# GpSimd takes over the softmax scalings and the recurrence tree's products in a hybrid decoder block

## The chip, the cores and the metric

The kernel runs on one core of one Trainium2 chip. Its time is device microseconds of one execution. A core has five engines with queues of their own, each worked off in order: TensorE (PE; its weight loads are shown as PEld), VectorE (DVE), ScalarE (ACT), GpSimd (POOL) and SyncE (SP), which only starts transfers here.

## What is computed

Two layers of a hybrid decoder over 256 tokens of width 1024, in float32. Each layer projects the normalized input, runs three groups of heads side by side, projects their outputs back and adds a squared-ReLU feed-forward. Cut to what matters here:

```python
for layer in range(DEPTH):
    h = _rmsnorm(x, norm1_g[layer])
    proj = h @ w_in[layer]
    o_a = _hgrn2(aq, af, ai, ag, ...)          # gated linear recurrence, 4 heads, 64x64 state
    o_b = _nsa(bq, bkc, bvc, ...)              # compressed + selected + window attention, 8 heads
    o_c = _fox(cq, ck, cv, cf, ...)            # forgetting attention, 4 heads
    x = x + concatenate([o_a, o_b, o_c]) @ w_o[layer]
    h2 = _rmsnorm(x, norm2_g[layer])
    x = x + square(relu(h2 @ w_up[layer])) @ w_down[layer]
...
# the recurrence: scores decayed by the product of the forget gates between s and t
decay = exp(where(causal, G[t] - G[s], NEG_BIG))         # G = cumsum(log f)
scores = einsum('bhtk,bhsk,bhtsk->bhts', q, k, decay)
...
# every softmax of the attention groups
p = where(mask, exp(logits - m), 0.0)
return p / maximum(sum(p), TINY)
```

## The kernel before

Tokens lie in two tiles of 128 partitions. Every large matmul is done as three passes over a high and a low part (`mm3`, lines 229 to 231), so each weight tile of 128x1024 is loaded (`raw`), copied to `whi` by ScalarE (line 223) and has its low part `wlo` subtracted by VectorE (line 224). A projection matmul below is one of these passes over 256 columns; a weight tile of the projections feeds 24 of them.

The recurrence is computed as a tree of seven levels, `a_level(0)` to `a_level(6)` (t0 to t6 below). Level `lv` multiplies queries and keys of neighbouring blocks of 2^lv tokens on TensorE into the one bank `pa` (line 470), which is emptied into `AT` by VectorE (line 479, under a mask) or, from level 5 on, by ScalarE (line 477). Then the queries `Qbd` are multiplied by the decays `Th` in two halves (line 485), the keys `Kc` once (line 487; `Kc` and the forget gates lie in buffers tagged `m2`, so the rows show `m`), and the decays themselves are paired for the next level (line 490). The next level's matmuls read the new `Qbd` and `Kc`. `a_out` ends the tree (lines 495 to 513).

The sparse attention group has heads b0 to b7, the forgetting group c0 to c3. A head's scores (lines 821 and 822, or 874 to 876) go through a masked maximum on VectorE (line 751) and an exponential with a running sum on ScalarE (line 161). The reciprocal sums, times the gates, are `rr`. `scale` then multiplies the probabilities `pt_` (buffers tagged `big0`, `big` in the rows) in place, in four pieces for a b head (two of 128 and two of 256 columns) and two for a c head (128 and 256). `SCALE_ACT` lists which pieces ScalarE scales (four of the six kinds), VectorE does the others. The scaled probabilities are transposed on TensorE (lines 836, 841, 884) into one of two banks `tr`, copied out and multiplied with the values (lines 858, 895). The compressed branch goes from `Z` and `w1` (line 613) over `hidT` (line 640) and `KC` (lines 652 to 659) to its scores (line 772).

The order of the steps in the program is the table `ORDER`, in which the tree's levels, the heads and the projections (`+ai`, `+q1`, ...) are mixed. What finally stands in each engine's queue is decided by the framework's list scheduler when the program is built: it follows that order as a priority and lets a later step go first where it reckons an earlier one is not ready. Where an operation sits on another engine, the scheduler reckons with another duration, and so the queues of all engines may come out in another order.

Of the kernel before, what the change touches and what calls it, by code (L numbers as in the profile page):

```python
# [13 lines left out]
AF = mybir.ActivationFunctionType  # L14
ALU = mybir.AluOpType
# [3 lines left out]
P = 128  # L19
# [38 lines left out]
WO_LAST = (0, 1, 2, 3)  # L58


WBUFS = (4, 6, 5)
SCALE_ACT = (1, 3, 4, 5)
CHUNK_N = {n: sum(b - a for a, b in c) for n, c in CHUNKS}
CHUNK_OFF = {}
_o = 0
# [70 lines left out]
def tile_block(ctx: ExitStack, tc: tile.TileContext, x_in, win, wo, wup, wdn, w1, vec, cst, out, dbg=None):  # L136
    nc = tc.nc
    V, A, G, PE = nc.vector, nc.scalar, nc.gpsimd, nc.tensor
# [31 lines left out]
    def T(shape, dt=F32, tag=None, bufs=1, pool=None):  # L170
        cnt[0] += 1
        return (pool or apool).tile(shape, dt, name=f"{tag}_{cnt[0]}", tag=tag, bufs=bufs)
# [3 lines left out]
    def bank(tag):  # L176
        return T([P, 512], F32, tag, BANKS[tag], pp)
# [163 lines left out]
    for L in range(DEPTH):  # L341
# [115 lines left out]
        th = [fT]  # L457

        def a_level(lv):


            Th = th[0]
            h = 1 << lv
            nb = S // (2 * h)
            ps = bank("pa")
            for t in range(2):
                for p in range(2):
                    o = (t * 2 + p) * P
                    mv = Qbd[:, p, :, t * P:(t + 1) * P].rearrange("p a (b two h) -> p a b two h", two=2, h=h)[:, :, :, 1, :]
                    PE.matmul(ps[:, o:o + P].rearrange("p (a b h) -> p a b h", a=2, h=h),  # L470
                              Kc[:, p, t * P:(t + 1) * P], mv, start=True, stop=True)
            atv = AT.rearrange("p a (b two h) -> p a b two h", two=2, h=h)[:, :, :, 1, :]
            psv = ps.rearrange("p (a b h) -> p a b h", a=8, h=h)
            if h >= 32:
                for b in range(64 // h):
                    r = slice(2 * h * b, 2 * h * b + h)
                    A.activation(atv[r, :, b, :], psv[r, :, b, :], AF.Copy)
            else:
                V.copy_predicated(
                    atv, hm[:, lv, :].rearrange("p (b h) -> p b h", h=h)[:, None, :, :].to_broadcast([P, 8, 64 // h, h]), psv)  # L480
            tv = Th.rearrange("p a (b two) -> p a b two", two=2)
            for a in range(2):
                r = slice(64 * a, 64 * a + 64)
                qv = Qbd[r, :, a, :].rearrange("p a (b two h) -> p a b two h", two=2, h=h)[:, :, :, 1, :]
                V.tensor_mul(qv, qv, tv[r, :, :, 0][:, :, :, None].to_broadcast([64, 2, nb, h]))
            kv = Kc.rearrange("p a (b two h) -> p a b two h", two=2, h=h)[:, :, :, 0, :]
            V.tensor_mul(kv, kv, tv[:, :, :, 1][:, :, :, None].to_broadcast([P, 2, nb, h]))
            if lv < 6:
                th[0] = T([P, 2, P], tag="Th", bufs=2)[:, :, :nb]
                V.tensor_mul(th[0], tv[:, :, :, 0], tv[:, :, :, 1])  # L490

        def a_out():
            ps = bank("pa")
# [254 lines left out]
        def softmax_part(ps, mask, n, ptile, o, nmx, sm):  # L748

            dst = ptile[:, o:o + n]  # L750
            V.tensor_tensor_reduce(out=dst, in0=ps, in1=mask, scale=-1.0, scalar=3.0e38,  # L751
                                   op0=ALU.add, op1=ALU.min, accum_out=nmx)
            act_exp(dst, dst, AF.Exp, bias=nmx, scale=-1.0, accum_out=sm)

        def scale(p, r, on_act):
            if on_act:
                A.activation(p, p, AF.Copy, scale=r)
            else:
                V.tensor_scalar(p, p, r, None, ALU.mult)

        PCT = [None, None]

# [49 lines left out]
        def head_b(g, j):  # L812
            hd = g * 4 + j
            pair, par = hd // 2, hd % 2
            pt_ = T([P, 768], tag="big0", bufs=4)
            nmx = T([P, 4], tag="nmx", bufs=4)
            sm = T([P, 4], tag="sm", bufs=4)
            for t, c0, n in ((0, P, 256), (1, 0, 512)):
                ps = bank("sc")
                sl = slice(t * P, (t + 1) * P)  # L820
                PE.matmul(ps[:, :n], qS[par][:, pair, sl], KS[:, g, c0:c0 + n], start=True, stop=False)
                PE.matmul(ps[:, :n], qS[par][:, pair, sl], KLB[:, g, c0:c0 + n], start=False, stop=True)
                w = n // 2
                for b, m in enumerate((tri, tri) if t == 0 else (m_tz, m_zt)):
                    i = 2 * t + b
                    softmax_part(ps[:, b * w:b * w + w], m, w, pt_, 256 * t + b * w, nmx[:, i:i + 1], sm[:, i:i + 1])
            r = T([P, 4], tag="rr", bufs=4)
            V.reciprocal(r, sm)
            rv = r.rearrange("p (t b) -> p t b", t=2)
            V.tensor_mul(rv, rv, gv[:, :, 1:3, g, j])  # L830
            for i, (o, n) in enumerate(((0, P), (P, P), (256, 256), (512, 256))):
                scale(pt_[:, o:o + n], r[:, i:i + 1], i in SCALE_ACT)

            ps0 = bank("tr")
            for i, o in enumerate((0, 384, P, 512)):
                PE.transpose(ps0[:, i * P:(i + 1) * P], pt_[:, o:o + P], ident)
            p0 = T([P, 2, S], tag="P0", bufs=3)
            A.activation(p0.rearrange("p b t -> p (b t)"), ps0, AF.Copy)
            ps1 = bank("tr")
            for i, o in enumerate((256, 640)):  # L840
                PE.transpose(ps1[:, i * P:(i + 1) * P], pt_[:, o:o + P], ident)
            p1 = T([P, 2, P], tag="P1", bufs=3)
            A.activation(p1.rearrange("p b t -> p (b t)"), ps1[:, 0:S], AF.Copy)
            PT[hd] = (p0, p1)
# [20 lines left out]
        def head_c(hd):  # L865
            u_, e_ = hd // 2, hd % 2
            pt_ = T([P, 768], tag="big0", bufs=4)
            nmx = T([P, 4], tag="nmx", bufs=4)
            sm = T([P, 4], tag="sm", bufs=4)
            for t in range(2):  # L870
                n = P * (t + 1)
                sl = slice(t * P, (t + 1) * P)
                ps = bank("sc")
                PE.matmul(ps[:, :n], cqS[e_][:, u_, sl], CK[:, hd, 0:n], start=True, stop=False)
                PE.matmul(ps[:, :n], cqS[e_][:, u_, sl], KLC[:, hd, 0:n], start=False, stop=False)
                PE.matmul(ps[:, :n], sel_r[:, hd:hd + 1].to_broadcast([P, P]), CC[:, 0:n], start=False, stop=True)  # L876
                softmax_part(ps[:, :n], tri if t == 0 else m_zt, n, pt_, t * P, nmx[:, t:t + 1], sm[:, t:t + 1])
            r = T([P, 4], tag="rr", bufs=4)
            V.reciprocal(r[:, 0:2], sm[:, 0:2])
            for t, (o, n) in enumerate(((0, P), (P, 256))):  # L880
                scale(pt_[:, o:o + n], r[:, t:t + 1], t + 4 in SCALE_ACT)
            ps0 = bank("tr")
            for i in range(3):
                PE.transpose(ps0[:, i * P:(i + 1) * P], pt_[:, i * P:(i + 1) * P], ident)
            p0 = T([P, 2, S], tag="P0", bufs=3)
            p0f = p0.rearrange("p b t -> p (b t)")
            A.activation(p0f[:, 0:384], ps0[:, 0:384], AF.Copy)
            PTC[hd] = p0f
# [55 lines left out]
        def wo_step(i):  # L944
# [12 lines left out]
        }  # L957
        step = {
            "t": a_level, "w": b_compress, "kc": b_compressed, "a_out": a_out,
            "cb": b_cmp_branch, "b": lambda i: head_b(i // 4, i % 4), "pb": lambda i: pv_b(i // 2, i % 2),  # L960
            "c": head_c, "pc": pv_c, "forget": c_forget, "wo": wo_step,
        }
        for name in ORDER:
# [163 lines left out]
```

## Time and profile before

| what | us |
|---|---|
| runs, median of 3 (lowest to highest) | 698.83 (697.93 to 699.84) |
| the profiled execution | 699.06 |
| its span, first to last instruction | 697.3 |
| mean granted TensorE clock | 0.993 of full |

The profile is of one execution. Its span begins with the first instruction of the program and ends with the last; the execution's own time is 1.8 us longer. In the rows, times are microseconds from the span's start. A mean granted clock below 1.00 in a stretch says that TensorE ran part of it at the lower of its two levels, 1.2 instead of 2.4 GHz. In rows of a timeline the first number is the start, the second the time taken, and brackets tell how long the engine stood idle before it and which work ended that.

### The profile page before, as it was taken

To read this page: it belongs to the slowest core of one execution; us is meant where nothing else is said; L and a number is where in the kernel's file an instruction comes from. 1 tells how busy PE (TensorE), PEld (TensorE's weight loads), DVE (VectorE), ACT (ScalarE), POOL (GpSimd) and SP (SyncE) were. 2 spreads that over 40 slices of the span, in tenths; PEclk is the share of its full clock that TensorE was granted. 3 is DMA by queue.
4 is the path that set the end of the run, shared out by engine and by line. 5 is a ranking of instruction groups with operands and counts; after the bars stand their busy time and mean duration, and the time that the engine had idled before them with its cause. 6 is when DMAs were issued, how large, how long until landed. Compare 5 with 4: busy or idle time off the path is not lost.

```text
span 697.3 us, 11902 instructions
## 1 busy us (share of the span) xinstructions
PE 675.9 (97%) x4578; PEld 602.4 (86%) x4578; DVE 451.6 (65%) x987; ACT 398.0 (57%) x761; POOL 10.9 (2%) x28
## 2 busy tenths in 40 slices
PE   6999989999999999999999999899999999999997
PEld 5998979768988998899799988786799988998896
DVE  5878788838655545654587897786567456545552
ACT  7654675887444434554457556688865445444440
POOL 3100000000100000000000000000000000000000
PEclk9999998999999999999999999999999999999999
DMA  8852561206566666666546418421266666666631
GB/s 289 265 153 73 174 189 49 73 1 211 168 203 181 181 185 183 192 182 194 153 128 213 150 31 260 133 62 31 86 190 180 184 191 196 180 185 181 185 118 61
DMA packets 31017, 108.88 MB, mean 156 GB/s; under 512 B 3568, under 2 KB 4080, under 8 KB 30960
## 3 DMA queue, kind: packets, MB, share of 16 engines
q1 hardware_dynamic: 30960, 108.11, 51.5%
q8 instruction: 36, 0.59, 0.3%
q14 instruction: 21, 0.17, 0.1%
HBM read 107.05 MB, written 1.05 MB: 155 GB/s over the span
## 4 chain that ended last, share of the span: by engine, by line
PE 82%; DVE 8%; ACT 5%; DMA 3%; issue 1%; SPq 0%; ACTq 0%
PE sc L229 9%; PE sc L230 9%; PE sc L231 9%; PE acc L229 9%; PE acc L231 8%; PE acc L230 8%; PE pv L230 3%; PE pv L231 3%; PE pv L229 3%; DMA raw<-in_win_dram 3%; PE pa L231 3%; PE pa L230 3%; PE pa L229 3%; DVE wlo L224 2%; PE pv L858 2%; PE sc L613 1%
## 5 line engine op out<-in xcount | busy, mean ns | idle before, releaser
L224 DVE TENSOR_TENSOR wlo<-raw,whi 128x1024 fp32r<-128x1024 f32 (+2 forms) x197 | 235.2, 1197 | 139.1 <-PE sc L231 67.2
L223 ACT ACTIVATE whi<-raw 128x1024 fp32r<-128x1024 f32 (+2 forms) x197 | 204.3, 1041 | 195.1 <-PE sc L230 73.3
L229 PE MATMUL sc<-kt,whi 128*128 128x256 f32 x512 | 145.1, 283 | 0.0
L231 PE MATMUL sc<-kt,wlo 128*128 128x256 f32 x512 | 144.9, 283 | 0.0
L230 PE MATMUL sc<-kt,whi 128*128 128x256 f32 x512 | 144.8, 283 | 0.0
L229 PEld LDWEIGHTS sc<-kt,whi 128*128 128x128 f32 x512 | 98.0, 191 | 1.0 <-ACT s L1015 0.3
L230 PEld LDWEIGHTS sc<-kt,whi 128*128 128x128 f32 x512 | 98.1, 192 | 0.6
L231 PEld LDWEIGHTS sc<-kt,wlo 128*128 128x128 f32 x512 | 98.1, 192 | 0.0
L229 PE MATMUL acc<-whi,kt 128*128 128x256 f32 (+2 forms) x288 | 88.9, 309 | 2.7 <-ACT whi L223 2.7
L231 PE MATMUL acc<-whi,kt 128*128 128x256 f32 (+2 forms) x288 | 88.4, 309 | 0.2
L230 PE MATMUL acc<-wlo,kt 128*128 128x256 f32 (+2 forms) x288 | 87.4, 305 | 0.0
L229 PEld LDWEIGHTS acc<-whi,kt 128*128 128x128 f32 x288 | 56.8, 197 | 5.3 <-ACT whi L223 3.3
L231 PEld LDWEIGHTS acc<-whi,kt 128*128 128x128 f32 x288 | 56.3, 196 | 3.3 <-DVE kt L239 1.1
L230 PEld LDWEIGHTS acc<-wlo,kt 128*128 128x128 f32 x288 | 56.3, 196 | 1.5 <-DVE wlo L224 0.4
L229 PE MATMUL acc<-whi,big 128*128 128x512 f32 x128 | 50.7, 396 | 0.0
L230 PE MATMUL acc<-wlo,big 128*128 128x512 f32 x128 | 50.6, 395 | 0.0
L231 PE MATMUL acc<-whi,big 128*128 128x512 f32 x128 | 50.5, 394 | 0.0
L161 ACT ACTIVATE big<-big,nmx 128x128 f32<-128x128 f32 (+1 forms) x80 | 35.6, 447 | 16.4 <-DVE nmx L751 16.3
L1016 DVE TENSOR_TENSOR s<-s 128x512 f32<-128x512 f32 x32 | 22.0, 688 | 24.1 <-ACT s L1015 24.1
L751 DVE CUSTOM_DVE_ANT_0 big<-sc,cst 128x128 f32<-128x128 f32 (+1 forms) x80 | 26.5, 349 | 8.0 <-PE sc L876 4.2
L1015 ACT ACTIVATE s<-sc 128x512 f32<-128x512 f32 x32 | 18.8, 588 | 18.7 <-PE sc L231 18.7
L231 PEld LDWEIGHTS acc<-whi,big 128*128 128x128 f32 x128 | 24.1, 188 | 5.8
(299 smaller groups left out, 1183.3 us busy)
## 6 DMA issues: line engine op xcount, KB each, us to landing
raw<-in_wup_dram SPq DMA_DIRECT2D x64, 512.0 KB, 3.6
raw<-in_wdn_dram SPq DMA_DIRECT2D x64, 512.0 KB, 3.6
raw<-in_win_dram SPq DMA_DIRECT2D x44, 512.0 KB, 4.5
raw<-in_wo_dram SPq DMA_DIRECT2D x16, 512.0 KB, 3.9
raw<-in_w_dram SPq DMA_DIRECT2D x8, 512.0 KB, 3.6
raw<-in_win_dram SPq DMA_DIRECT2D x4, 426.0 KB, 3.7
out_dram<-x SPq DMA_DIRECT2D x4, 256.0 KB, 2.0
raw<-in_win_dram SPq DMA_DIRECT2D x2, 284.0 KB, 2.7
```

What stands on the lines that cost most here:

```text
L161: r = A.activation(*a, **k)
L223: A.activation(hi[:, c0], raw[:, c0], AF.Copy)
L224: V.tensor_sub(lo[:, c0], raw[:, c0], hi[:, c0].bitcast(F32))
L229: PE.matmul(ps, ah, wh, start=start, stop=False)
L230: PE.matmul(ps, ah, wl, start=False, stop=False)
L231: PE.matmul(ps, al, wh, start=False, stop=stop)
L613: PE.matmul(pre_[0][64 * w:64 * w + 35, 0:P], Z[:, w].rearrange("p g m -> p (g m)")[:, j:j + 273:8], raw1[w][:, c0:c0 + P], start=(j == 0) ...
L751: V.tensor_tensor_reduce(out=dst, in0=ps, in1=mask, scale=-1.0, scalar=3.0e38, op0=ALU.add, op1=ALU.min, accum_out=nmx)
L858: PE.matmul(po[64 * e_:64 * e_ + 64, t * P:S], VS[:, t, bi * 2 + g, :], PT[g * 4 + jj * 2 + e_][t][:, bi, :], start=False, stop=False)
L1015: A.activation(rl, pu[i], AF.Relu)
L1016: V.tensor_mul(rl, rl, rl)
```

## The change

`scale` always uses GpSimd, for all 24 heads of both layers; the list `SCALE_ACT` goes. In `a_level` the two products on `Qbd`, the one on `Kc` and the one that pairs the decays go from VectorE to GpSimd. Nothing else of the source changes.

```diff
 WBUFS = (4, 6, 5)
-SCALE_ACT = (1, 3, 4, 5)
...
-                V.tensor_mul(qv, qv, tv[r, :, :, 0][:, :, :, None].to_broadcast([64, 2, nb, h]))
+                G.tensor_mul(qv, qv, tv[r, :, :, 0][:, :, :, None].to_broadcast([64, 2, nb, h]))
...
-            V.tensor_mul(kv, kv, tv[:, :, :, 1][:, :, :, None].to_broadcast([P, 2, nb, h]))
+            G.tensor_mul(kv, kv, tv[:, :, :, 1][:, :, :, None].to_broadcast([P, 2, nb, h]))
             if lv < 6:
                 th[0] = T([P, 2, P], tag="Th", bufs=2)[:, :, :nb]
-                V.tensor_mul(th[0], tv[:, :, :, 0], tv[:, :, :, 1])
+                G.tensor_mul(th[0], tv[:, :, :, 0], tv[:, :, :, 1])
...
-        def scale(p, r, on_act):
-            if on_act:
-                A.activation(p, p, AF.Copy, scale=r)
-            else:
-                V.tensor_scalar(p, p, r, None, ALU.mult)
+        def scale(p, r):
+            G.tensor_scalar(p, p, r, None, ALU.mult)
...
-                scale(pt_[:, o:o + n], r[:, i:i + 1], i in SCALE_ACT)
+                scale(pt_[:, o:o + n], r[:, i:i + 1])
...
-                scale(pt_[:, o:o + n], r[:, t:t + 1], t + 4 in SCALE_ACT)
+                scale(pt_[:, o:o + n], r[:, t:t + 1])
```

Since the list scheduler orders all queues anew, instructions move on TensorE, VectorE and ScalarE too; SyncE's queue stays as it was. In the changed kernel a line's number is lower by two up to `scale` and by five behind it (the tree's matmuls are L468 there, the scores L816 and L817, the heads' transposes L831 and L836, the `w1` matmuls L611). Three places in layer 0 are shown; layer 1 has the same order.

TensorE from t2 (bank pa_848) to t3 (pa_859), before; 22 projection matmuls and the four score matmuls of head b2 stand between t1 and t2, and all the rows left out are projection matmuls:

```order
L470 MATMUL pa_848<-Qbd_74,m_41_175 128x128 x4
L821 MATMUL sc_917<-KS_77,qS_179 128x256
L822 MATMUL sc_917<-KLB_78,qS_179 128x256
L230 MATMUL acc_984<-wlo_988,kt_16_100 128x256
L231 MATMUL acc_984<-whi_987,kt_17_101 128x256
...
L821 MATMUL sc_924<-KS_77,qS_179 128x512
L822 MATMUL sc_924<-KLB_78,qS_179 128x512
...
L470 MATMUL pa_859<-Qbd_74,m_41_175 128x128 x4
L836 MATMUL tr_902<-cst_70,big_156_878 128x128
```

The same place in the changed kernel; before the first row stand 8 projection matmuls and the four score matmuls of head b2 since t1:

```order
L468 MATMUL pa_848<-Qbd_74,m_41_175 128x128 x4
L229 MATMUL acc_984<-whi_987,kt_17_101 128x256
L227 MATMUL acc_984<-whi_987,kt_16_100 128x256
L228 MATMUL acc_984<-wlo_988,kt_16_100 128x256
L816 MATMUL sc_917<-KS_77,qS_179 128x256
L817 MATMUL sc_917<-KLB_78,qS_179 128x256
...
L468 MATMUL pa_859<-Qbd_74,m_41_175 128x128 x4
L816 MATMUL sc_924<-KS_77,qS_179 128x512
L817 MATMUL sc_924<-KLB_78,qS_179 128x512
L611 MATMUL sc_950<-raw_951,Z_177 35x128
```

Fourteen projection matmuls went from before t2 to behind the tree, and t3 moved up: between t2 and t3 six projection matmuls and one pair of scores are left, between t3 and t4 one pair of scores and eight of line 613.

TensorE around t4 (pa_963) before; between the rows left out stand only matmuls of line 613, and the transposes of the next head, b1 (tr_938), come only after t4, behind eight projection matmuls:

```order
L836 MATMUL tr_902<-cst_70,big_156_878 128x128
L613 MATMUL sc_950<-raw_951,Z_177 35x128
L836 MATMUL tr_902<-cst_70,big_156_878 128x128 x3
L841 MATMUL tr_909<-cst_70,big_156_878 128x128 x2
...
L470 MATMUL pa_963<-Qbd_74,m_41_175 128x128 x4
```

The same place in the changed kernel:

```order
L468 MATMUL pa_963<-Qbd_74,m_41_175 128x128 x2
L831 MATMUL tr_902<-cst_70,big_156_878 128x128
L468 MATMUL pa_963<-Qbd_74,m_41_175 128x128
L831 MATMUL tr_902<-cst_70,big_156_878 128x128 x3
L836 MATMUL tr_909<-cst_70,big_156_878 128x128 x2
L468 MATMUL pa_963<-Qbd_74,m_41_175 128x128
L611 MATMUL sc_950<-raw_951,Z_177 35x128
L831 MATMUL tr_938<-cst_70,big_166_914 128x128
...
L831 MATMUL tr_938<-cst_70,big_166_914 128x128 x3
L836 MATMUL tr_945<-cst_70,big_166_914 128x128 x2
```

The transposes of both heads now stand inside and right behind t4, with three matmuls of line 613 between them; 34 projection matmuls follow five more of line 613.

GpSimd from the products of t3 to those of t4 in the changed kernel (before, its queue holds nothing between the tables of rotations of layer 0, `tabc`, and those of layer 1):

```order
L483 TENSOR_TENSOR Qbd_74<-Qbd_74,Th_857 64x2x16x8 x2
L485 TENSOR_TENSOR m_41_175<-m_41_175,Th_857 128x32x8
L488 TENSOR_TENSOR Th_972<-Th_868 128x2x8
L754 TENSOR_SCALAR big_156_878<-big_156_878,rr_895 128x128 x2
L754 TENSOR_SCALAR big_156_878<-big_156_878,rr_895 128x256 x2
L754 TENSOR_SCALAR big_166_914<-big_166_914,rr_931 128x128 x2
L754 TENSOR_SCALAR big_166_914<-big_166_914,rr_931 128x256 x2
L483 TENSOR_TENSOR Qbd_74<-Qbd_74,Th_868 64x2x8x16 x2
```

The eight scalings of heads b2 and b1 stand between t3's products and t4's; they came here from VectorE's and ScalarE's queues, the products from VectorE's.

## Rows read from the trace of the kernel before

**Rows 1.** The page's busy times: us (share of the span) xinstructions of each engine.

```profile
PE 675.9 (97%) x4578; PEld 602.4 (86%) x4578; DVE 451.6 (65%) x987; ACT 398.0 (57%) x761; POOL 10.9 (2%) x28
```

**Rows 2.** TensorE's waits over the whole span: us in total, times, longest.

```profile
PE sc L640 <- DVE hidT L638: 2.7, 2, 1.5
...
PE sc L772 <- DVE KC L659: 2.3, 2, 1.1
PE pa L470 <- DVE m L487: 1.9, 3, 0.7
PE tr L841 <- ACT P L838: 1.4, 2, 0.7
PE tr L652 <- DVE s L552: 0.8, 2, 0.4
```

**Rows 3.** Stretches: length, busy time of each engine, granted clock, DMA share, GB/s.

```profile
105.00:125.00 20.00, 19.69 (x128) 17.21 (x128) 16.96 (x69) 12.44 (x33) 0.00 (x0) 0.83 0.26 81
125.00:140.00 15.00, 14.95 (x86) 11.32 (x86) 11.91 (x54) 13.65 (x44) 0.00 (x0) 1.00 0.12 35
...
440.00:460.00 20.00, 17.78 (x130) 16.50 (x128) 16.99 (x68) 12.31 (x33) 0.00 (x0) 0.91 0.26 79
```

**Rows 4.** Timeline of TensorE, layer 0, from t1 to the compressed branch's scores.

```profile
61.83 1.14 PE L470 MATMUL pa<-Qbd,m 128*128 128x128 f32 x8 [0.67 <-DVE m L487]
62.72 0.37 PE L229 MATMUL acc<-whi,kt 128*128 128x256 f32 x1
62.93 0.28 PE L230 MATMUL acc<-wlo,kt 128*128 128x256 f32 x1
63.05 0.28 PE L231 MATMUL acc<-whi,kt 128*128 128x256 f32 x1
...
66.82 1.13 PE L470 MATMUL pa<-Qbd,m 128*128 128x128 f32 x8 [0.53 <-DVE m L487]
...
73.73 1.16 PE L470 MATMUL pa<-Qbd,m 128*128 128x128 f32 x8
...
77.81 1.98 PE L613 MATMUL sc<-raw,Z 128*35 128x128 f32 x32
79.72 1.16 PE L470 MATMUL pa<-Qbd,m 128*128 128x128 f32 x8
...
92.04 1.03 PE L495 MATMUL pa<-Qbd,m 128*128 128x256 f32 x4
...
104.98 1.89 PE L772 MATMUL sc<-KC,qS 128*128 128x32 f32 x8 [1.13 <-DVE KC L659]
```

**Rows 5.** Timeline of VectorE, layer 0: t1's last product, and t4's bank.

```profile
66.25 0.42 DVE L487 TENSOR_TENSOR m<-m,Th 128x256 f32<-128x256 f32 x1
...
74.93 0.72 DVE L479 COPY_PREDICATED AT<-hm,pa 128x512 f32<-128x512 uint8 x1 [0.38 <-PE pa L470]
```

**Rows 6.** ScalarE's scalings, line 757: durations (ns min/median/max), and who waited (us, times).

```profile
L757 ACT ACTIVATE big<-big,rr x48: 385/448/511, 70.6 to 496.3; 128x128 f32<-128x128 f32 x24, 128x256 f32<-128x256 f32 x24
...
  PEld tr L836: 3.0, 8
  PEld tr L884: 0.8, 2
```

**Rows 7.** Timeline of GpSimd over the whole span.

```profile
2.52 0.31 POOL L207 MEMSET LF<- 128x256 f32 x1
2.77 0.21 POOL L207 MEMSET hidT<- 128x128 f32 x1
...
17.48 1.38 POOL L935 TENSOR_TENSOR tabk<-cst,vec 128x64 f32<-128x64 f32 x1
...
177.73 0.32 POOL L935 TENSOR_TENSOR tabk<-cst,vec 128x64 f32<-128x64 f32 x1
178.01 0.25 POOL L939 TENSOR_TENSOR tabc<-cst,vec 64x32 f32<-64x32 f32 x1
```

**Rows 8.** Timeline of VectorE from 15.5 us: weight subtractions beside GpSimd's product.

```profile
17.47 2.48 DVE L224 TENSOR_TENSOR wlo<-raw,whi 128x1024 fp32r<-128x1024 f32 x2
```

## Prediction

> **What bounds the kernel now.** I read the page's busy times first. TensorE is busy 675.9 of 697.3 us, VectorE 451.6, ScalarE 398.0, GpSimd 10.9 [rows 1]. So the span is TensorE's work plus what it waits, and no edit off TensorE can win more than TensorE's idle time and what a low clock costs it. Where that lies is read from stretches, not from the mean. The edits touch the two attention parts alone, about 60 to 160 us in layer 0 and 400 to 500 in layer 1.
>
> Inside, three things stand out. The longest waits of TensorE over the whole run, two of each (one a layer) or three, are for `hidT` (2.7 us), `KC` (2.3), the tree's `Kc` (`m` in the rows, 1.9), a bank that ScalarE empties (1.4) and the compressed keys' rotation (0.8) [rows 2]: 9.1 us, all ended by VectorE or ScalarE. Second, the granted clock is 0.83 over 105 to 125 us and 0.91 over 440 to 460 [rows 3]. With levels of 1.2 and 2.4 GHz these means stand for 2 x 0.17 x 20 = 6.8 us and 2 x 0.09 x 20 = 3.6 us at the lower one, which cost half of it, 3.4 and 1.8 us. Both come right behind the places where TensorE stood waiting for `KC`. Third, ScalarE is busy 13.65 of 15 us from 125 to 140 [rows 3], where the attention heads are worked off.
>
> **What the change removes.** From VectorE 42 tree multiplications of 128 or 64 partitions by 256 at 0.42 us [rows 5], 17.6 us, the tree's 12 smaller products and 32 scalings; from ScalarE 48 scalings at 0.448 us, 21.5 us [rows 6]. None of it is TensorE's, so it is worth only the waits that it ends. Those that can be read directly: transposes waited 3.0 + 0.8 = 3.8 us for ScalarE's scalings [rows 6]. I count this 3.8 as won: GpSimd has nothing else in the heads' stretch, and the scalings leave the queue that is full there.
>
> **What it adds.** Two prices are not in the rows as such.
>
> A multiplication of 256 elements on GpSimd: two undisturbed ones took 0.32 us for 64 elements and 0.25 for 32 [rows 7], so 0.07 / 32 = 2.2 ns an element on 0.18, and 0.74 us for 256. Back to back one starts 0.28 after a 0.32 one, so three take 0.70 + 0.70 + 0.74 = 2.14 us. Lower bound: VectorE's own 0.42 each, 1.27 in all. Upper: four times 0.32, 1.28, if none of that were a fixed part. I take 0.74, from the same operation on the same engine.
>
> A scaling: fills of 128 and 256 columns took 0.21 and 0.31 us [rows 7], which bounds a head of four (two of 128, two of 256) below at 1.04 us; the two-input line gives 0.46 and 0.74, so 2.4 us above. A scaling reads one tensor, where a fill reads none and a product two, so I take the middle, 1.7 a head.
>
> **The tree, walked through layer 0.** A level's matmuls occupy TensorE 0.89 us (61.83 to 62.72) and end 1.14 after their start; other projection matmuls follow at 0.12 us each (62.93, 63.05) [rows 4]. VectorE starts 0.04 after a level's end, and TensorE 0.15 after the last product (66.25 + 0.42, then 66.82) [rows 4, 5]. So with GpSimd one level can follow the last after 1.14 + 0.04 + 2.14 + 0.15 = 3.47 us. Today VectorE needs about as long, since it empties the level's bank first; that goes on beside GpSimd. What is different is the order: TensorE has less work laid between levels.
> - t1: today it waits 0.67 behind a full VectorE [rows 4]; GpSimd has nothing in front of t0's products. It starts at 61.2.
> - t2: between t1 and t2 stand 0.89 + 8 projection matmuls (0.96) + scores (0.7) = 2.5 us, so 0.9 idle; t2 at 64.7 (today 66.82).
> - t3: 0.89 + 6 x 0.12 + 0.23 = 1.8, so 1.6 idle; t3 at 68.1.
> - t4: 0.89 + 0.46 + 8 x 0.12 (line 613: 1.98 for 16 [rows 4]) = 2.3, so 1.1 idle; t4 at 71.6.
> - Heads b2 and b1 now stand right behind t4, and their eight scalings queue on GpSimd behind t3's products and a small product (to 71.7): 71.7 + 2 x 1.7 = 75.1, and the last transposes end at 75.5. Between 73 and 75.5 TensorE waits about 1.5 us.
> - Then 5 of L613 (0.6), 34 projection matmuls (4.1) and 16 of L613 (1.9): 82.1, where today it is 79.72 [rows 4]. The tree is 2.4 us late.
> - t5, L622 and 27 projection matmuls: 86.5. `hidT` is ready after its VectorE chain, which stands behind the same two weight tiles, so I leave its 1.4 us of waiting; then 0.8 and 21 projection matmuls with scores (3.0): t6 at 91.7. Behind t6 only 14 projection matmuls stand (1.7 + 0.89), so L495 waits 0.9 and starts at 95.15. Today it starts at 92.04, and 0.46 us of scores come after it that now come before: 2.65 late.
> - From L495 to L772 today takes 12.94 us (to 104.98) [rows 4]. In it lie the 0.46 us of scores that now come earlier, and three waits: 0.4 at L652, 0.7 at L841 and 1.1 at L772 (half of each in [rows 2]). The order now puts L772 eleven projection matmuls (1.3 us) earlier among this work, and L652 and the transposes beside it are covered by the output matmuls of the tree. The `KC` chain begins with L640, which now starts 7 us ahead of L495 (87.9 to 95.15) and today only four projection matmuls and one pair of scores ahead of it, and VectorE has less in its queue, so I count none of the three waits: 12.94 - 0.46 - 2.2 = 10.3 us.
>
> Sum at the same work done: 95.15 + 10.3 = 105.45 against 104.98, +0.5. The late tree and the ended waits nearly cancel; I book +0.6 a layer.
>
> **The clock.** If TensorE no longer stands still around L652 to L772, the low stretch behind it may go: 3.4 + 1.8 = 5.2 us. But the new order makes TensorE idle about 40% of the time from 64 to 75.5. I book half, 2.6.
>
> **The sum.** 697.3 + 2 x 0.6 - 2.6 - 3.8 = 692.1 us of span. The profiled execution took 699.06, 1.8 more than its span, and the median of the runs is 698.83, 0.2 below it: 693.7.
>
> **One rule against it.** A product of 64 elements that took 0.32 us undisturbed took 1.38 at 17.48 us, while two weight subtractions of VectorE ran from 17.47 for 2.48 us [rows 7, 8]: one collision costs 1.06 us. The Trainium skill, SBUF — State Buffer, section "Who interferes with whom", says that a VectorE instruction with two SBUF inputs and a GpSimd one that reads SBUF exclude each other for a whole instruction, whichever is second; by that rule the trace agrees. From t1 to t4 the new order lays no weight subtraction on VectorE, so the walk above is untouched; t6 and everything behind it is not.
>
> **The rivals.**
> - *Slower: GpSimd's product is dearer than 0.74 us.* The place is the twelve products that gate t2, t3, t4 and L495. Each extra 0.1 us costs 1.2 us a layer, 2.4 in all. The gain of 5.2 is gone at 0.96 us; at 1.1, two thirds of the way to the upper bound, with dear scalings (+1.4 a layer for b2 and b1) it is +2 x (4.3 + 1.4) and the low clock stays: 697.3 + 11.4 + 1.2 - 3.8 = 706 of span, 707. For it: the line hangs on two small products, none with the tree's strides, and TensorE's order leaves no slack. Against: the line through two rows. 0.24.
> - *No change: collisions at t6.* Three products before L495, each caught by one weight subtraction: 3.2 us a layer, 6.4: 700. Some of that is hidden by tiles waiting anyway; with the low clock gone, 698. 0.14.
> - *A larger gain.* The products last 0.42 us (then each of the four chains is 0.9 us shorter, up to 3.6 a layer), or the low clock goes in both layers and the heads' stretch closes up, because ScalarE's 21.5 us were queued in front of its exponentials: 2.6 more and another 4. Either way about 687. For it: 13.65 of 15 us. Against: TensorE is busy 14.95 of 15 there. 0.20.
> - *The forecast*, 690 to 696.7: 0.42.
>
> A measurement of this kernel can tell about 0.3% (2.1 us) from no change. Faster is the forecast and the larger gain, 0.62; same 0.14; slower 0.24. The range goes from 685, just beyond the larger gain, to 705, which leaves out the dearest products.
>
> **What would show it.** In the changed profile GpSimd should be busy near 11 + 42 x 0.74 + 4 for the smaller products + 20 x 1.7 for the scalings (a FoX head has half the columns) = 80 us; a tree product of 256 elements should last 0.7 to 0.8 us between 60 and 75 us; TensorE should wait for GpSimd at t2, t3 and t4 for 0.9, 1.6 and 1.1 us; the wait for `KC` should be gone and with it the 0.83 clock; ScalarE should be busy 376 us. The prediction is wrong if those products take 1 us or more, if the clock falls in the tree, or if the heads' transposes wait for GpSimd longer than they did for ScalarE.

## The result and the profile after

The changed kernel is slower: 733.07 us median of 4 runs (730.8 to 736.29) against 698.53 for the kernel before on the same chip, a ratio of 1.0495 with a 95% interval of 1.0453 to 1.0538. The forecast was 693.7, so even the direction was wrong.

The page's span and busy times after, which answer to [rows 1]:

```profile
span 731.4 us, 11941 instructions
...
PE 688.3 (94%) x4578; PEld 607.1 (83%) x4578; DVE 435.1 (59%) x901; ACT 383.5 (52%) x713; POOL 117.3 (16%) x162
```

VectorE's busy time fell by 16.5 us and ScalarE's by 14.5 (to 383.5, where the list of signs said 376). GpSimd is busy for 117.3 us where that list said 80, and TensorE, with the same 4578 matmuls, is busy 12.4 us longer, which goes with the clock below. TensorE's waits after, which answer to [rows 2]:

```profile
PE tr L831 <- POOL big L754: 19.8, 29, 1.9
PE pa L468 <- POOL m L485: 5.2, 6, 1.3
...
PE pa L493 <- POOL m L485: 3.3, 2, 1.8
PE tr L879 <- POOL big L754: 3.1, 5, 0.8
...
PE sc L638 <- DVE hidT L636: 0.7, 2, 0.3
```

The old waits, for `KC`, for the tree's `m` from VectorE, for the emptied bank and for the rotation, are no longer among the longest, and the one for `hidT` is down from 2.7 to 0.7. In their place TensorE waits 22.9 us for scalings on GpSimd (L831 and L879) and 8.5 for the tree's products (L468 and L493). Of the 22.9, only 2.9 lie in the tree; 20.0 lie behind the compressed branch's scores, in the stretch of the other heads. What makes the waits for scalings so long is in GpSimd's groups, by shape (busy us, mean ns of one):

```profile
L754 POOL TENSOR_SCALAR big<-big,rr 128x256 f32<-128x256 f32 x40 | 41.7, 1051 | 0.0
L754 POOL TENSOR_SCALAR big<-big,rr 128x128 f32<-128x128 f32 x40 | 28.2, 712 | 86.7 <-DVE rr L825 44.4 <-ACT rs_yA L159 26.5 <-DVE rr L874 15.8
L483 POOL TENSOR_TENSOR Qbd<-Qbd,Th 64x256 f32<-64x256 f32 x24 | 17.1, 713 | 38.2 <-PE pa L468 37.3
L485 POOL TENSOR_TENSOR m<-m,Th 128x256 f32<-128x256 f32 x12 | 8.7, 722 | 0.9
```

A scaling of 256 columns takes 1.05 us on average, longer than a product of two tensors of that size (0.72, last row). A b head's four come to 2 x 1.05 + 2 x 0.71 = 3.5 us on average. Where this meets the tree is seen on GpSimd's timeline in layer 0:

```profile
69.09 1.36 POOL L483 TENSOR_TENSOR Qbd<-Qbd,Th 64x256 f32<-64x256 f32 x2 [0.98 <-PE pa L468]
70.53 0.64 POOL L485 TENSOR_TENSOR m<-m,Th 128x256 f32<-128x256 f32 x1
71.25 0.23 POOL L488 TENSOR_TENSOR Th<-Th 128x16 f32<-128x16 f32 x1
71.45 5.99 POOL L754 TENSOR_SCALAR big<-big,rr 128x128 f32<-128x128 f32 x8
77.42 1.32 POOL L483 TENSOR_TENSOR Qbd<-Qbd,Th 64x256 f32<-64x256 f32 x2
```

and on TensorE's, which answers to [rows 4]:

```profile
60.81 1.07 PE L468 MATMUL pa<-Qbd,m 128*128 128x128 f32 x8
64.40 1.16 PE L468 MATMUL pa<-Qbd,m 128*128 128x128 f32 x8 [0.55 <-POOL m L485]
67.85 1.16 PE L468 MATMUL pa<-Qbd,m 128*128 128x128 f32 x8 [1.33 <-POOL m L485]
...
71.22 0.71 PE L468 MATMUL pa<-Qbd,m 128*128 128x128 f32 x4 [0.71 <-POOL m L485]
72.13 0.33 PE L831 MATMUL tr<-cst,big 128*128 128x128 f32 x1 [0.20 <-POOL big L754]
...
73.62 0.69 PE L831 MATMUL tr<-cst,big 128*128 128x128 f32 x2 [0.93 <-POOL big L754]
...
86.37 1.16 PE L468 MATMUL pa<-Qbd,m 128*128 128x128 f32 x8
```

Up to t4 TensorE comes at the times forecast (61.2, 64.7, 68.1, 71.6). Then the transposes of b2 and b1 wait for eight scalings, which take 6.0 us, and TensorE reaches t5 at 86.37 instead of the forecast 82.1. TensorE's idle time there is only 1.3 us (0.20 and 0.93 above, and 0.21 for one more transpose at 74.52): the matmuls between take longer. The clock goes with it (stretches of two us; the number before the last two is the granted clock):

```profile
72.00:74.00 2.00, 0.94 (x5) 0.66 (x5) 0.69 (x6) 0.00 (x0) 2.00 (x4) 0.89 0.00 0
74.00:76.00 2.00, 1.79 (x8) 1.24 (x7) 0.12 (x1) 0.87 (x2) 2.00 (x4) 0.50 0.02 4
76.00:78.00 2.00, 2.00 (x10) 1.06 (x9) 0.98 (x3) 0.00 (x0) 2.00 (x3) 0.50 0.00 0
```

0.50 is the lower level, 1.2 GHz, and ahead of it TensorE was busy for 0.94 of 2 us. At that level ten matmuls fill the 2 us from 76. It stays so to 80 us. The low clock comes back in the heads' stretch, from 138 to 146 us and from 150 to 166.

**Where the 34.1 us of span went.** Waits for scalings are 22.9 us and for products 8.5. The waits that ended are 2.3 + 1.9 + 1.4 + 0.8 and 2.0 of `hidT`, 8.4. The mean granted clock is 0.977 of 731.4 us, which costs 0.023 x 731.4 = 16.8 us; before it was 0.993 of 697.3, 4.9. So 22.9 + 8.5 - 8.4 + 11.9 = 34.9, close to the 34.1 measured. The page's own figures say the same: TensorE is busy 12.4 us longer and idle for 43.1 us, where it was 21.4.

**Where in a layer it went.** Here a heads' stretch is counted from the first matmul of the compressed branch's scores to the first of the feed-forward. The rows are layer 0 and layer 1, before and then after:

```profile
104.98:169.41 64.43, 63.77 (x379) 49.52 (x380) 45.02 (x164) 49.92 (x137) 0.00 (x0) 0.95 0.24 71
447.41:510.67 63.26, 62.59 (x378) 48.14 (x379) 44.95 (x164) 49.93 (x137) 0.00 (x0) 0.97 0.24 72
...
107.85:187.21 79.36, 70.03 (x391) 53.05 (x390) 45.40 (x155) 46.58 (x123) 24.76 (x28) 0.89 0.21 61
468.85:544.73 75.88, 64.75 (x391) 49.26 (x390) 45.25 (x155) 46.47 (x123) 24.69 (x28) 0.98 0.22 64
```

The two stretches grew by 14.9 and 12.6 us, 27.5 of the 34.1 in all, and TensorE is idle for 20.5 us of them, where it was for 1.3. Everything up to the compressed scores, the tree with it, lost only 6.5 in both layers. So the scenes above show how a wait arises; most of the loss lies behind the tree, in the heads' stretch.

### The profile page after: what moved, and what is told of

It is laid out like the page before. It is cut to its first block, busy times and chain, and to the rows that moved or that the text cites. A ratio compares the mean times of both kernels' runs of the same rounds, so it can differ in the third digit from the quotient of the medians.

```text
span 731.4 us, 11941 instructions
## 1 busy us (share of the span) xinstructions
PE 688.3 (94%) x4578; PEld 607.1 (83%) x4578; DVE 435.1 (59%) x901; ACT 383.5 (52%) x713; POOL 117.3 (16%) x162
## 3 DMA queue, kind: packets, MB, share of 16 engines
HBM read 107.05 MB, written 1.05 MB: 148 GB/s over the span
## 4 chain that ended last, share of the span: by engine, by line
PE 81%; POOL 8%; DVE 4%; ACT 4%; issue 1%; DMA 1%; SPq 0%; POOLq 0%; ACTq 0%
PE acc L229 9%; PE acc L227 9%; PE acc L228 9%; PE sc L227 8%; PE sc L228 8%; PE sc L229 8%; POOL big L754 7%; PE pv L228 3%; PE pv L229 3%; PE pv L227 3%; PE pa L227 3%; PE pa L228 2%; PE pa L229 2%; PE pa L468 2%; PE pv L853 2%
## 5 line engine op out<-in xcount | busy, mean ns | idle before, releaser
L754 POOL TENSOR_SCALAR big<-big,rr 128x128 f32<-128x128 f32 (+1 forms) x80 | 69.2, 882 | 86.7 <-DVE rr L825 44.4
L831 PE MATMUL tr<-cst,big 128*128 128x128 f32 x64 | 18.6, 348 | 20.2 <-POOL big L754 19.8
```

Source lines behind the costliest of these rows:

```text
L754: G.tensor_scalar(p, p, r, None, ALU.mult)
```

## Experiments

Theory A says that the scalings are the loss: they are dearer than reckoned, GpSimd does a head's four one behind the other, and TensorE's transposes stand right behind them. Theory B blames the tree's products, theory C the new order of the queues whatever things last. D came later and blames the meeting of both parts on GpSimd inside the tree. Each kernel was timed beside the kernel before on its own chip, so excesses over that kernel are compared. In the traces, e3 has the instructions of the changed kernel in the same order on all four engines, and e6 those of e5. Every other edit but e7's also made the list scheduler order TensorE's queue anew, so these runs change more than the line shown.

| run | us | kernel before | ratio (95%) |
|---|---|---|---|
| e1, scalings alone | 729.17 | 698.0 | 1.0453 (1.0435 to 1.0471) |
| e2, tree alone | 692.69 | 698.0 | 0.9925 (0.9910 to 0.9940) |
| e3, scalings as two-input products | 709.55 | 698.0 | 1.0158 (1.0139 to 1.0177) |
| e4, no scaling | 688.42 | 698.0 | 0.9865 (0.9850 to 0.9879) |
| e5, later transposes | 711.46 | 698.47 | 1.0179 (1.0151 to 1.0206) |
| e6, later transposes, two-input | 702.48 | 698.47 | 1.0047 (1.0027 to 1.0068) |
| e8, tree and VectorE's scalings | 697.39 | 698.47 | 0.9988 (0.9978 to 0.9997) |
| e9, tree without `Kc` | 690.4 | 697.36 | 0.9896 (0.9878 to 0.9913) |
| e10, `Kc` and pairing alone | 693.19 | 697.36 | 0.9936 (0.9921 to 0.9951) |
| e11, b1 and b2 scaled as before | 711.33 | 697.36 | 1.0197 (1.0178 to 1.0216) |
| e12, tree and the c heads' scalings | 693.88 | 697.36 | 0.9947 (0.9929 to 0.9965) |

### The two parts apart: e1 and e2

e1 is the changed kernel with its four `G.tensor_mul` of `a_level` as `V.tensor_mul`.

> Only the 80 scalings on GpSimd; the tree's products are back on VectorE. Theory A (the scalings: a b head's four take 3.0 us undisturbed where 1.7 was reckoned, and TensorE's transposes stand right behind them): most of the 34 us stays, 718 to 730, and TensorE's waits for the scalings remain at 15 to 23 us. Theory B (the tree's products are what costs): 696 to 704, since TensorE waited 8.5 us for them.

e2 is the kernel before with the edit of `a_level` alone.

> Only the tree's products on GpSimd; the scalings are split between ScalarE and VectorE as before. Theory A: within 5 us of before, 694 to 703, since a product takes 0.61 to 0.66 us undisturbed. Theory B: 715 to 730. If both parts cost by themselves, the excesses of this run and of the one with the scalings alone add up to 34 us.

e1 loses 31.2 us, as theory A expected, and e2 wins 5.3, which is 1.3 us below theory A's range. Theory B falls: the part that it blames makes the kernel faster by itself. TensorE's waits for scalings in e1 are 13.2 + 4.0 = 17.2 us, and its clock is 0.979. VectorE, which has the tree again, keeps TensorE waiting 5.1 us for the compressed keys' rotation. TensorE's waits in e2:

```profile
PE pa L470 <- POOL m L487: 5.2, 6, 1.4
...
PE pa L495 <- POOL m L487: 2.3, 2, 1.2
...
PE tr L836 <- ACT big L757: 1.9, 2, 1.0
```

TensorE waits 7.5 us for GpSimd's products here too, and the waits for `KC`, `hidT` and the tree's `m` from VectorE are gone. These nearly cancel: its idle time is 22.5 us, where it was 21.4. What is won is busy time, 668.1 us in place of 675.9, and the mean granted clock is 1.00. The excesses do not add up: 31.2 - 5.3 = 25.9, while both together cost 34.5. The 8.6 us between them are taken up in e11.

### Price against order: e3

```diff
-            G.tensor_scalar(p, p, r, None, ALU.mult)
+            G.tensor_mul(p, p, r.to_broadcast([P, p.shape[1]]))
```

> The changed kernel, with the scalings on GpSimd written as a product of two tensors (the factor repeated along the columns) in place of a multiplication by one factor a partition. All five queues keep the order of the changed kernel, so only the duration of 80 instructions differs. If a two-input product takes 0.61 us for 256 and 0.40 for 128 as in the tree, a b head's four take 2.0 us instead of 3.0. Theory A (their duration): TensorE's waits for them fall from 22.9 us by a third or more and the time to 710 to 724. Theory C (the new order of the queues costs, whatever a scaling lasts): 729 to 736, the same.

709.55 us, half a us below theory A's range. The excess over the kernel before is 11.5 us in place of 34.5, so 23.0 came back, with every queue in the same order. GpSimd's two groups:

```profile
L754 POOL TENSOR_TENSOR big<-big,rr 128x256 f32<-128x256 f32 x40 | 28.8, 734 | 0.0
...
L754 POOL TENSOR_TENSOR big<-big,rr 128x128 f32<-128x128 f32 x40 | 16.5, 428 | 90.6 <-DVE rr L825 61.7 <-DVE rr L874 14.7 <-ACT rs_yA L159 14.3
```

GpSimd does 69.9 - 45.3 = 24.6 us less of scaling. That this is near the 23.0 won is chance, since the gain has two parts of about the same size. TensorE's waits for scalings fall from 22.9 to 8.7 + 1.6 = 10.3 us, the clock's cost from 16.8 to 0.006 x 710.3 = 4.3. Theory C as stated falls. The kernel is still 11.5 us slower than before. In its trace the heads' two stretches take 69.27 us each, together 10.9 more than before, of the 13.0 by which its span is longer. So what is left lies where most of the loss lay.

### The ceiling: e4

In e4 the line of `scale` is `pass`.

> The changed kernel with the scaling of the probabilities left out (they go into the transposes unscaled); the tree's products stay on GpSimd. It is the ceiling for anything done about the scalings. Theory A: 688 to 700. Theory B: over 710, since the tree's products still gate TensorE and the clock still falls in the tree.

688.42 us, at the lower end of theory A's range. The span is 686.9 against 690.6 of e2: with the queues in another order too, scalings that cost nothing at all, on any engine, are worth 3.7 us. So little was to be won by moving them.

### Place in TensorE's queue: e5 and e6

Each head's transposes become a step of their own (`tb2` for b2, `tc0` for c0), placed later in `ORDER`; e6 has e3's line besides:

```diff
-         "b1", "w0", "t4", "w1", "cv", "+ai", "w2", "w3", "ai", "t5", "kc", "b0", "+q1", "q1", "cb0", "t6", "b3",
+         "b1", "w0", "t4", "w1", "cv", "tb2", "+ai", "w2", "tb1", "w3", "ai", "t5", "kc", "b0", "+q1", "tb0", "q1", "cb0", "t6",
...
+            PTB[hd] = pt_
+
+        def tr_b(hd):
+            pt_ = PTB[hd]
             ps0 = bank("tr")
```

> The changed kernel with each head's transposes made a step of its own, placed one or two steps later in the order table, so that TensorE has projection matmuls or the next head's scores between a head's scalings and its transposes; the scalings stay as dear as in the changed kernel. Theory A in its narrow form (the 22.9 us that TensorE waited for scalings, and the low clock behind them, are the loss): waits for scalings under 8 us, 698 to 715. Rival (GpSimd is full in the heads' stretch, so that its queue gates them wherever they stand): 722 to 734.

> The same later transposes, and the scalings as two-input products of 0.43 and 0.73 us. Theory A: waits for scalings near nothing, 688 to 698. Rival (the tree's and heads' steps of the new order cost by themselves): no better than 705.

e5 takes 711.46 us with scalings nearly as dear as in the changed kernel (0.99 and 0.62 us). The waits for them are 9.5 + 0.3 us, a little over the 8 expected; the time is in the range of theory A. So most of the same loss goes away by either of two edits, cheaper scalings or other work ahead of the transposes, which is what theory A asks. From e5 to e6, whose queues are the same, only the price falls, and another 9.0 us go with it: a second clean test of the price. e6 misses both expectations all the same. Its waits for scalings are only 1.0 us, but 702.48 us remain. Its other waits:

```profile
PE pa L468 <- POOL m L485: 5.2, 6, 1.3
PE sc L638 <- DVE hidT L636: 4.9, 2, 2.5
...
PE acc L227 <- DVE s L542: 2.2, 2, 1.1
...
PE tr L836 <- POOL big L754: 1.0, 2, 0.5
```

A wait for `hidT` of 4.9 us came in (1.3 in e5, with the same queues), and in the profiled execution, which took 703.23 us, the clock is 0.991, where e2 has 1.00: 0.009 x 701.4 = 6.3 us. In the other four it is 0.992 to 0.997. e3 and e6 have the same price and other queues, and e6 is some 7 us faster, so the order matters too. But e6's order is its own: that the changed kernel's order costs by itself, as theory C says, is not shown. What made `hidT` late was not looked into.

### The price by itself: e7

The kernel before, with this behind its last tile, three times for 128 and for 256 columns (`x` and the factor `sc` lie in SBUF):

```diff
+                    G.tensor_scalar(d_, s_, sc[:, 0:1], None, ALU.mult)
+                    G.tensor_scalar(d_, d_, 0.5, None, ALU.mult)
+                    G.tensor_mul(d_, d_, sc[:, 0:1].to_broadcast([P, n]))
+                    G.tensor_mul(d_, d_, s_)
+                    G.tensor_copy(d_, s_)
```

> The kernel before, with 30 GpSimd instructions behind its last feed-forward tile, alone on their engine and without VectorE or ScalarE work beside them: a multiplication by one factor a partition, by a constant, a product with the factor repeated along the columns, a product of two full tensors, and a copy, each three times for 128 and for 256 columns. If the form sets the price: factor 0.60 and 0.85 us or more, two-input 0.40 and 0.61. If the 1.05 us of the changed kernel is contention: factor no dearer than two-input here. The time of the run says nothing (some 20 us more).

GpSimd's groups of those lines (L1074 to L1078 in that order; busy us, mean ns of one):

```profile
L1074 POOL TENSOR_SCALAR s<-x,rr 128x256 f32<-128x256 f32 x3 | 2.7, 922 | 0.0
L1075 POOL TENSOR_SCALAR s<-s 128x256 f32<-128x256 f32 x3 | 2.5, 847 | 0.0
L1077 POOL TENSOR_TENSOR s<-s,x 128x256 f32<-128x256 f32 x3 | 2.1, 722 | 0.0
L1076 POOL TENSOR_TENSOR s<-s,rr 128x256 f32<-128x256 f32 x3 | 1.8, 612 | 0.0
L1074 POOL TENSOR_SCALAR s<-x,rr 128x128 f32<-128x128 f32 x3 | 1.8, 604 | 514.5 <-DVE rr L1069 514.5
...
L1076 POOL TENSOR_TENSOR s<-s,rr 128x128 f32<-128x128 f32 x3 | 1.2, 398 | 0.0
L1078 POOL COPY s<-x 128x256 f32<-128x256 f32 x3 | 1.1, 399 | 0.0
```

The form sets the price. With nothing beside it, the multiplication by one factor a partition takes 0.92 and 0.60 us: a b head's four are 3.05 us. Of the changed kernel's mean of 1.05, then, 0.92 is the instruction. The 0.13 left may be disturbance by other engines; no run isolates it. The run's own time is not compared. The Trainium skill, GPSIMD Engine Reference, section "Engine selection", says that GpSimd is about two times slower than VectorE for two-input operations and that one-input ones are roughly at line rate. For this form the measurement differs and decides: one input and a factor took 0.92 us, two full tensors 0.72, while VectorE scaled the same pieces in at most 0.36 us (before, L759).

### Fewer scalings on GpSimd: e8, e11 and e12

e8 is e2 with VectorE's share of the scalings (32 of 80) as two-input products on GpSimd:

```diff
-                V.tensor_scalar(p, p, r, None, ALU.mult)
+                G.tensor_mul(p, p, r.to_broadcast([P, p.shape[1]]))
```

> The tree's products on GpSimd, ScalarE's scalings as before, and of the scalings only those that VectorE did (32 of 80) on GpSimd, as two-input products. Theory A: a b head's two scalings on GpSimd take 1.2 us beside ScalarE's two of 0.9 us, so nothing is later than with VectorE, and VectorE gets 10 us back: 688 to 694, near 692.7 or below. Rival (any scaling on GpSimd makes transposes late): 697 to 705.

697.39 us: the rival's range, so theory A's expectation missed. VectorE has less to do, but TensorE waits 3.9 us for these scalings, the longest 1.24. GpSimd's timeline at that wait in layer 0:

```profile
72.88 1.33 POOL L485 TENSOR_TENSOR Qbd<-Qbd,Th 64x256 f32<-64x256 f32 x2 [1.13 <-PE pa L470]
74.29 0.63 POOL L487 TENSOR_TENSOR m<-m,Th 128x256 f32<-128x256 f32 x1
74.99 0.20 POOL L490 TENSOR_TENSOR Th<-Th 128x8 f32<-128x8 f32 x1
75.15 0.97 POOL L759 TENSOR_TENSOR big<-big,rr 128x128 f32<-128x128 f32 x2
```

Two cheap scalings of head b1 come behind the tree's products. Their factor is ready at 74.23 us on VectorE, so the queue makes them 0.9 us late, and their price is not at fault there. It explains little of the loss, though: in e2 TensorE waits 1.0 us in the same place for ScalarE's scalings, and e8's span is 4.4 us longer than e2's. More of that, 3.1 us, lies in the heads' stretches (63.00 us each against 61.43 and 61.44), and what causes it there is open.

e11 is the changed kernel with two heads left to ScalarE and VectorE:

```diff
-                scale(pt_[:, o:o + n], r[:, i:i + 1])
+                scale(pt_[:, o:o + n], r[:, i:i + 1], i if hd in (1, 2) else None)
```

> The changed kernel, but heads b1 and b2, whose scalings lie between the tree's levels, are scaled by ScalarE and VectorE as before; all other heads by GpSimd. The scalings alone cost 31 us, the products alone won 5, together they cost 34.5: 8.5 us more than the sum. Theory D (that is the meeting of both on GpSimd within the tree: t4's products stood behind eight scalings): TensorE comes to t5 6 us earlier in each layer, and the time is 717 to 723. Rival (the meeting costs nothing, the loss sits in the later heads): 727 to 733.

711.33 us, 21.7 less than the changed kernel (20.6 by the excesses), more than theory D expected. TensorE comes to t5 at 82.34 us instead of 86.37, 4.0 us earlier and not 6. The clock is 0.995 against 0.977, 0.005 x 709.1 = 3.5 us instead of 16.8. From 60 to 180 us the clock is 1.00, through layer 0's heads' stretch too, whose scalings were not edited (0.90 in the changed kernel); from 420 to 545, in layer 1, it is 0.97, little more than the 0.96 there. So two heads of twelve carry more than half of the loss.

The traces divide it. In e11 the parts up to the compressed scores are 8.5 us shorter than in the changed kernel, the heads' two stretches (69.81 and 71.69 us) 13.7. Theory D's account of the 8.6 us doesn't fit: up to the compressed scores both parts together lose 6.5 us, less than the 9.7 that e1 and e2 make in sum (+11.5 and -1.8). In the heads' stretches they lose 27.5, where e1 and e2 make 13.8 (+18.6 and -4.8). So what the parts cost beyond their sum lies behind the tree, not in it. Why it goes when b1 and b2 are scaled as before is open: the clock and the new order of the queues both changed.

e12 is e2 with the c heads' two scalings as two-input products on GpSimd, where ScalarE did both.

> The kernel with only the tree's products on GpSimd, and the forgetting heads' scalings (two a head, 16 in all) moved to GpSimd as two-input products of about 0.40 and 0.62 us, where ScalarE did both. Theory A: 1.0 us on an empty GpSimd against 0.9 us behind others on ScalarE: 690 to 695, no difference that can be told. Rival (any scaling on GpSimd makes the transposes late): 696 to 702.

693.88 us, in theory A's range and as e2 within the intervals: where GpSimd is empty, cheap scalings cost nothing that can be told, and win nothing.

### Which product of the tree: e9 and e10

e9 is e2 with `Kc`'s product back on VectorE, e10 e2 with the two on `Qbd` there:

```diff
-            G.tensor_mul(kv, kv, tv[:, :, :, 1][:, :, :, None].to_broadcast([P, 2, nb, h]))
+            V.tensor_mul(kv, kv, tv[:, :, :, 1][:, :, :, None].to_broadcast([P, 2, nb, h]))
```

> The kernel with only the tree's products on GpSimd, with the one on Kc given back to VectorE. In that kernel TensorE waited 7.5 us for the tree's three products in a row (1.36 us for the two halves of Qbd, then 0.64 for Kc). Theory A (GpSimd's serial products are what still gates the tree): Kc's 0.42 us runs beside the halves, up to 0.6 us less for each of eight waits, 688 to 692. Rival (VectorE is behind its bank copy and the maxima, or the two engines hold each other up): 692 to 697.

> The same, but the two halves of Qbd are VectorE's and Kc and the pairing of the decays GpSimd's. Theory A: VectorE has 0.84 us behind its bank copy of 0.72, GpSimd 0.64 beside them; 688 to 694. Rival (VectorE is what made the tree late in the kernel before): 694 to 698.

e9 is the fastest version of all that compute the whole: 690.4 us, in theory A's range, 1.0% below the kernel before and some 42 us below the changed one. Its TensorE timeline:

```profile
60.53 1.07 PE L470 MATMUL pa<-Qbd,m 128*128 128x128 f32 x8
64.31 1.13 PE L470 MATMUL pa<-Qbd,m 128*128 128x128 f32 x8 [0.38 <-DVE m L487]
...
67.09 1.16 PE L470 MATMUL pa<-Qbd,m 128*128 128x128 f32 x8
69.87 1.16 PE L470 MATMUL pa<-Qbd,m 128*128 128x128 f32 x8
```

A level now follows the last after 2.78 us (64.31 to 67.09 to 69.87), where with all three on GpSimd it took 3.45. The interval overlaps e2's, so that e9 is faster than e2 is likely and not settled; that both are faster than before is. e10, 693.19, lies in theory A's range (688 to 694) and cannot be told from e2. TensorE waits 4.9 us in it for VectorE's `s` (L544), which is not among e2's longest waits. On the same chip e9 is 2.8 us faster than e10, clear of the intervals, so `Kc`'s product is the better one to give back.

## Why the prediction was wrong

**The step that failed** is the term for the heads: "I count this 3.8 as won: GpSimd has nothing else in the heads' stretch". It let scalings there cost TensorE nothing. Measured, the two heads' stretches grew by 27.5 us, with 20.0 us of waiting for scalings in them. The step counted GpSimd's load and not its latency: TensorE's transposes wait for four serial scalings, where before two engines shared them, at 0.45 us each on ScalarE. The 3.8 itself was no idle time of TensorE's: [rows 6] has it as waits of weight loads (`PEld`), which overlap matmuls (86% and 97% of the span in [rows 1]), and among TensorE's own waits before none for a scaling is listed. That e4 against e2 shows 3.7 us as the most that free scalings could give is luck.

**The price failed with it:** "A scaling reads one tensor, where a fill reads none and a product two, so I take the middle, 1.7 a head." It takes 3.05 us alone (e7) and 3.5 on average in the kernel, beyond the upper bound of 2.4. That bound came from the two-input product, as if one input could not be dearer than two. The ordering by inputs was an assumption, and no row of before showed a multiplication by a factor on GpSimd. e3 prices the mistake: 80 instructions at 2.3 a head and nothing else changed give back 23.0 of the 34.5 us. The right price alone would not have saved the forecast, since the sum charges it only to b2 and b1: 2 x (3.05 - 1.7) = 2.7 us a layer, an estimate of 692.1 + 5.4 = 697.5 of span, no change. And at a price within the prediction's bounds e3 is still 11.5 us slower than before, most of it in the heads' stretches.

**The step that was right and was drowned** is the walk through the tree. The product was forecast at 0.74 us; with collisions it takes 0.71 on average, and 0.64 where nothing meets it (at 70.53 us in the timeline above). t1 to t4 came within 0.4 us of the forecast in the changed kernel. In e11, where the heads b1 and b2 are not scaled on GpSimd, t5 comes at 82.34 and L493 at 94.59 (forecast 82.1 and 95.15), and in e2 at 82.03 and 94.29. That is in part luck, as the forecast held 1.5 us of waiting for these scalings on GpSimd; e11 waits 0.96 us there for one on VectorE instead. The wait for `KC` went, as forecast, and with it the low clock behind it: e2 has 1.00, so it won all 4.9 us of the clock's cost, where half of 5.2 was booked. With the tree alone the booked sum would have been 697.3 + 1.2 - 2.6 = 695.9 of span; measured were 690.6, 5.3 less, 2.3 of it by the clock. Where the other 3.0 come from was not traced.

**The eight scalings behind t4.** The prediction saw them ("their eight scalings queue on GpSimd"), charged 2 x 1.7, and let TensorE wait about 1.5 us. They took 6.0 us. By the same walk the last of them, ending at 77.4 instead of 75.1, puts t5 at about 84.4; it came at 86.37, and the other 2.0 us go with the clock of 0.50 from 74 to 80. That t4's own products then stood behind the scalings until 77.42 was not charged at all, though nothing waited for those in the end: TensorE was still later.

**The clock.** "the new order makes TensorE idle about 40% of the time from 64 to 75.5. I book half" treated a fall in the tree as a smaller gain, never as a loss. It fell there, at 74 us, and later at the heads: 11.9 us of the 34. In e11 two heads less on GpSimd bring layer 0's clock back far behind them, layer 1's hardly. That TensorE's standing still is what lowers the clock is read from where the low stretches begin; no run isolates it. Nor do the rows settle it: ahead of the fall at 138 us TensorE was busy for 2.05 of 4 us, but in e11 it was busy for 2.17 of 4 us from 134 and for 1.81 of 4 from 146, and the clock stayed at 1.00.

**The rivals.** "Slower: GpSimd's product is dearer" had the sign and, in its aside "with dear scalings (+1.4 a layer...)", the right thing at a tenth of its size. Its own mechanism did not occur. The collision at t6 did: the two `Qbd` products there took 2.35 us (from 96.54) instead of the 1.31 of t5 while VectorE subtracted a weight tile (from 97.19, 1.23 us), and L493 waits 1.51 instead of 0.9. The Trainium skill, SBUF — State Buffer, section "Who interferes with whom", which the prediction weighed, agrees with that, at 1.0 us in layer 0.

## What to carry to other kernels

Price an instruction by a row of its own form; where the trace has none, an upper bound taken from another form is no bound, and a two-line measurement is cheap. For an engine that feeds TensorE in order, count the latency from the last input to the first transpose, and what TensorE has to do meanwhile; the engine's free time alone says nothing about that. Read from a wait row which engine waited: a waiting weight load is not yet an idle TensorE. Where a chain has several products, try moving only some of them, so that two engines work side by side (e9).

## What the hardware showed unexpectedly

On GpSimd a multiplication by one factor a partition takes 0.92 us for 128 x 256 and the same result as a product with the factor repeated along the columns 0.61, with a copy at 0.40; from 128 to 256 columns that is 2.5, 1.7 and 0.9 ns a column. And the lower clock can go far from the edit: with only the two heads in the tree scaled as before, layer 0's low stretches at 138 to 166 us went too, by what way is not shown.
